# Ten of 22 feed-forward tile pairs by Strassen's seven products, and the inner width in three parts

## The chip, the cores and the metric

The kernel runs on one core of a Trainium2 chip. The metric is the device time of one execution in microseconds; the time before is the median of three runs.

## The reference, cut to what matters

The input has 512 positions of width 1024. A first block (three mixers and a convolutional feed-forward) is followed by a second block of two layers. Each of these layers has a feed-forward, a mixing stage and another feed-forward, so that the gated feed-forward below is computed four times, with an inner width `D_FF` of 2816:

```python
def _swiglu(x, w_in, w_out):
    a, b = jnp.split(x @ w_in, 2, axis=-1)
    return (jax.nn.silu(a) * b) @ w_out

n = _modulate(_rmsnorm_2(h, norm_g[l, 0]), mod[:, 0, 0], mod[:, 0, 1])
h = h + 0.5 * mod[:, 0, 2] * _swiglu(n, ffn_w_in[l, 0], ffn_w_out[l, 0])
# ... mixing stage ...
n = _modulate(_rmsnorm_2(h, norm_g[l, 2]), mod[:, 2, 0], mod[:, 2, 1])
h = h + 0.5 * mod[:, 2, 2] * _swiglu(n, ffn_w_in[l, 1], ffn_w_out[l, 1])
```

`mod` is a product of a conditioning vector with a large matrix, and `_modulate(xn, shift, scale)` is `xn * (1 + scale) + shift`.

## The kernel before

Activations lie with features on the 128 partitions and 512 tokens along the free axis, as 8 chunks (`KD`) of 128 features. Each float32 product is made of three matmuls: both operands are split into a high and a low part, and `mm3` (L275) adds high by high (L277), high by low (L278) and low by high (L279). A weight tile of 128 outputs comes by `weight` (L262): SyncE issues a 512 KB transfer into one of three `raw` buffers, ScalarE rounds it to `hi` (L268), VectorE subtracts for `lo` (L272); `hi` and `lo` have four buffers each. `dense` (L281) multiplies such a tile by all 512 tokens: 8 chunks x 3 = 24 matmuls of 512 columns.

`swiglu` (L729) norms its input into `xh` and `xl`, and then goes through the 22 tile pairs (`NF`) of the inner width: a gate tile and a value tile by `dense`, Silu on ScalarE (L740), the product on VectorE (L741), and the split into chunk f of `hh` and `hl` (L344, L346). The first two pairs come by `dense_halves` (L292), which does the first 256 tokens for all four weight tiles and then the other 256, so that work can start when the norm of the first half is there. When all 22 chunks stand, `outputs` (L303) makes the 8 output tiles over 22 chunks each, and adds them to the residual `res` through the gate (L726). The last output tile (the last two where there are at most 8 chunks) is done by token halves, and between them stand the reductions and the `rsqrt` chain of the next norm's first half (`part`, L465): the per-token sums of squares (L425), some ten small VectorE operations (L375 to L400) and the spread of the result over the partitions (L433). `scaled` (L489) then applies the next norm: per chunk and half one product into `nm` (L498), a high part on ScalarE (L503) and a low part on VectorE (L504). In the first feed-forward `joint_norm` (L755) also scales the residual itself (L766).

The modulation matrix is read in 144 tiles of 512 KB; each is one VectorE operation (L1436). They are queued in `self.mods`, and `filler` pops some between other work with a low priority. In `swiglu` one is popped for each pair, and two for each of the first five output tiles.

The order of the instructions on each engine is made by the framework's scheduler: a lower program position goes first, an instruction that could run goes before one that still waits, and waits are put where data or buffers need them. PSUM has three banks of tag `acc`, two of `s`, two of `t` and one of `o`.

## Time and profile before

| | us |
|---|---|
| median of three runs | 3364.63 (3364.01 to 3367.19) |
| the profiled execution | 3369.15 |
| its span | 3367.0 |
| TensorE busy (share of the span) | 3289.3 (98%) |
| VectorE busy | 1902.2 (56%) |
| ScalarE busy | 1345.2 (40%) |
| GpSimd busy | 133.5 (4%) |

The profile is of one execution. A busy time is the union of an engine's instructions; matmuls overlap in the records, so that the distance of two starts, not a duration, is the price of one. The four feed-forwards of the second block begin at about 1091, 1859, 2228 and 2987 us of the span and take some 365 us each. In a row of a timeline the first number is the start and the second the duration, in us; a name such as `acc<-xh,hi` gives the output, the moving operand and the weights.

### The profile page before, as it was taken

To read this page: it belongs to the slowest core of one execution; us is meant where nothing else is said; L and a number is where in the kernel's file an instruction comes from. 1 tells how busy PE (TensorE), PEld (TensorE's weight loads), DVE (VectorE), ACT (ScalarE), POOL (GpSimd) and SP (SyncE) were. 2 spreads that over 40 slices of the span, in tenths; PEclk is the share of its full clock that TensorE was granted. 3 is DMA by queue.
4 is the path that set the end of the run, shared out by engine and by line. 5 is a ranking of instruction groups with operands and counts; after the bars stand their busy time and mean duration, and the time that the engine had idled before them with its cause. 6 is when DMAs were issued, how large, how long until landed. Compare 5 with 4: busy or idle time off the path is not lost.

```text
span 3367.0 us, 43228 instructions
## 1 busy us (share of the span) xinstructions
PE 3289.3 (98%) x16598; PEld 2739.1 (81%) x16598; DVE 1902.2 (56%) x3598; ACT 1345.2 (40%) x2363; POOL 133.5 (4%) x152
## 2 busy tenths in 40 slices
PE   8999998899999999999999999999999999999998
PEld 6779777688888888897887888898888878888887
DVE  6757685777764644458556644454444775553333
ACT  4646664444433332247632322232222673232221
POOL 0000121000000000021000000000000200000000
PEclk9999999999999999999999999999999999999999
DMA  5351225444454444431245444434443212523332
GB/s 176 96 147 36 80 91 176 155 150 160 134 168 132 132 144 143 138 113 51 73 127 189 138 138 147 142 124 144 144 149 124 81 57 85 174 89 95 99 93 71
DMA packets 143641, 412.89 MB, mean 123 GB/s; under 512 B 27749, under 2 KB 32677, under 8 KB 142922
## 3 DMA queue, kind: packets, MB, share of 16 engines
q1 hardware_dynamic: 142248, 408.02, 38.1%
q8 instruction: 130, 2.13, 0.3%
q0 software_dynamic: 896, 1.87, 0.2%
q14 instruction: 77, 0.63, 0.1%
q10 hardware_dynamic: 290, 0.24, 0.0%
HBM read 383.06 MB, written 27.01 MB: 122 GB/s over the span
## 4 chain that ended last, share of the span: by engine, by line
PE 85%; DVE 5%; ACT 4%; DMA 2%; issue 1%; POOL 0%; SPq 0%; DVEq 0%; ACTq 0%; POOLq 0%
PE acc L277 24%; PE acc L278 24%; PE acc L279 24%; PE o L822 2%; PE s L783 1%; PE t L810 1%; ACT hi L268 1%; PE s L278 1%; PE s L277 1%; PE s L279 1%; DMA raw<-in_ada_dram 1%; DVE lo L272 1%; PE t L425 1%; ACT sq L1507 1%; DMA gt<-gd 1%
## 5 line engine op out<-in xcount | busy, mean ns | idle before, releaser
L277 PE MATMUL acc<-xh,hi 128*128 128x512 f32 (+1 forms) x2872 | 1084.5, 381 | 13.9 <-ACT gst L627 3.6
L268 ACT ACTIVATE hi<-raw 128x1024 fp32r<-128x1024 f32 (+2 forms) x529 | 541.5, 1025 | 1388.9 <-PE acc L278 1279.1
L278 PE MATMUL acc<-xl,hi 128*128 128x512 f32 (+1 forms) x2872 | 1089.9, 382 | 4.7 <-DVE xl L348 3.1
L279 PE MATMUL acc<-xh,lo 128*128 128x512 f32 (+1 forms) x2872 | 1087.0, 381 | 0.5 <-DVE lo L272 0.5
L272 DVE TENSOR_TENSOR lo<-raw,hi 128x1024 fp32r<-128x1024 f32 (+2 forms) x493 | 590.2, 1198 | 476.9 <-ACT hi L268 453.6
L277 PEld LDWEIGHTS acc<-xh,hi 128*128 128x128 f32 x2872 | 541.5, 190 | 116.8 <-ACT gst L627 5.6
L278 PEld LDWEIGHTS acc<-xl,hi 128*128 128x128 f32 x2872 | 543.4, 190 | 105.2 <-issue 5.3
L279 PEld LDWEIGHTS acc<-xh,lo 128*128 128x128 f32 x2872 | 542.9, 189 | 98.6 <-issue 4.0
L1436 DVE CUSTOM_DVE_ANT_0 raw<-raw,sc,vp 128x1024 f32<-128x1024 f32 x144 | 184.8, 1284 | 274.9 <-DMA raw<-in_ada_dram 274.4
L279 PE MATMUL acc<-hh,lo 128*128 128x512 f32 (+1 forms) x880 | 338.0, 384 | 0.0
L278 PE MATMUL acc<-hl,hi 128*128 128x512 f32 (+1 forms) x880 | 334.5, 380 | 0.0
L277 PE MATMUL acc<-hh,hi 128*128 128x512 f32 (+1 forms) x880 | 333.0, 378 | 0.0
L278 PEld LDWEIGHTS acc<-hl,hi 128*128 128x128 f32 x880 | 165.2, 188 | 37.9
L277 PEld LDWEIGHTS acc<-hh,hi 128*128 128x128 f32 x880 | 165.1, 188 | 34.7
L279 PEld LDWEIGHTS acc<-hh,lo 128*128 128x128 f32 x880 | 165.5, 188 | 33.3
L741 DVE TENSOR_TENSOR g<-g,acc 128x512 f32<-128x512 f32 x84 | 57.8, 688 | 219.1 <-PE acc L279 218.4
L270 POOL TENSOR_TENSOR lo<-raw,hi 128x1024 fp32r<-128x1024 f32 (+3 forms) x36 | 77.2, 2148 | 2093.5 <-ACT hi L268 1982.5
L726 DVE SCALAR_TENSOR_TENSOR res<-acc,mod,res 128x512 f32<-128x512 f32 (+1 forms) x48 | 33.9, 707 | 116.0 <-PE acc L279 116.0
L346 DVE TENSOR_TENSOR ptl<-t,pth 128x512 fp32r<-128x512 f32 (+3 forms) x148 | 81.6, 567 | 26.8 <-ACT pth L344 26.1
L787 ACT ACTIVATE pr<-pr,mx 128x128 f32<-128x128 f32 (+3 forms) x160 | 88.5, 555 | 15.6 <-DVE mx L786 14.8
L344 ACT ACTIVATE pth<-t 128x512 fp32r<-128x512 f32 (+3 forms) x148 | 70.7, 497 | 44.5 <-PE t L810 37.1
L786 DVE CUSTOM_DVE_ANT_0 pr<-s,cm 128x128 f32<-128x128 f32 (+3 forms) x160 | 74.5, 485 | 22.2 <-PE s L783 17.7
(522 smaller groups left out, 4167.1 us busy)
## 6 DMA issues: line engine op xcount, KB each, us to landing
raw<-in_w_in_dram SPq DMA_DIRECT2D x176, 512.0 KB, 3.6
raw<-in_ada_dram SPq DMA_DIRECT2D x144, 512.0 KB, 3.5
raw<-in_w_out_dram SPq DMA_DIRECT2D x64, 512.0 KB, 3.6
raw<-in_w_mix_dram SPq DMA_DIRECT2D x56, 512.0 KB, 3.5
raw<-in_w_up_dram SPq DMA_DIRECT2D x44, 512.0 KB, 3.7
gd<-gst SPq DMA_DIRECT2D x56, 256.0 KB, 2.0
gt<-gd SPq DMA_DIRECT2D x56, 256.0 KB, 3.2
raw<-in_w_gate_dram SPq DMA_DIRECT2D x24, 512.0 KB, 4.3
```

What stands on the lines that cost most here:

```text
L268: self.last_act = nc.scalar.activation(hi[:, :n], raw[:, :n], AF.Copy)
L270: nc.gpsimd.tensor_sub(lo[:, :n], raw[:, :n], hi[:, :n].bitcast(F32))
L272: nc.vector.tensor_sub(lo[:, :n], raw[:, :n], hi[:, :n].bitcast(F32))
L277: return [mm(acc, ahi, bhi, start=start, stop=False, **kw), mm(acc, ahi, blo, start=False, stop=False, **kw), mm(acc, alo, bhi, start=Fals ...
L278: mm(acc, ahi, blo, start=False, stop=False, **kw),
L279: mm(acc, alo, bhi, start=False, stop=stop, **kw)]
L344: nc.scalar.activation(hi, src, AF.Copy, scale=scale)
L346: nc.vector.tensor_sub(lo, src, hi.bitcast(F32))
L786: nc.vector.tensor_tensor_reduce(p, ps[:, :w], mask(i), -scale, 3.0e38, op0=OP.add, op1=OP.min, accum_out=mx[:, i:i + 1])
L787: nc.scalar.activation(p, p, AF.Exp, bias=mx[:, i:i + 1], scale=-1.0, accum_out=sm[:, i:i + 1])
L822: nc.tensor.matmul(acc[:, j * P:], x, m, start=start and j == 0 and k == 0, stop=stop and j == 3 and k == len(ops) - 1)
L1436: nc.vector.tensor_tensor_reduce(w, w, self.sc, 1.0, self.v("ada_b_2", l * 72 + n), op0=OP.mult, op1=OP.add, accum_out=self.mod[:, l, n:n ...
```

## The change

In each of the four feed-forwards the inner width is cut into three parts of 8, 8 and 6 chunks (`PARTS`). After each part its down products run at once over that part's chunks and are added to the residual, so that `hh` and `hl` have 8 chunks instead of 22. Where a part isn't the last, each of its 8 output tiles is made by `dense`, and two modulation tiles are popped behind each; none are popped in the pairs any more. The last part goes through `outputs`, over 6 chunks, which brings it under the rule for two output tiles in halves.

Of the 22 pairs, those with odd f from 3 on (ten) go through `seven`. It takes the gate and the value tile as a two by two block matrix (gate or value, first or second four chunks of the input) and the input as another (chunks, token halves), and makes Strassen's seven products of half size: 4 chunks by 256 columns each, 12 matmuls. Sums of the weights are made on VectorE in the `raw` buffers, sums of the input once for a feed-forward in `sums`, from the normed values that `scaled` now leaves in `xb` (`keep`). Combining the products takes two banks of `s` and two of `t` and further VectorE operations.

```diff
@@ scaled
             for k in range(n):
-                if b - a == S or k % 2 == 0:
-                    m2 = self.t(self.np_, [P, S], F32, "nm", 2)
-                m = m2 if b - a == S else m2[:, k % 2 * (b - a):(k % 2 + 1) * (b - a)]
+                if self.keep is not None:
+                    m = self.keep(k, a)
+                else:
+                    if b - a == S or k % 2 == 0:
+                        m2 = self.t(self.np_, [P, S], F32, "nm", 2)
+                    m = m2 if b - a == S else m2[:, k % 2 * (b - a):(k % 2 + 1) * (b - a)]
@@ swiglu
+    PARTS = ((0, 8), (8, 16), (16, 22))
+    PLAIN = 3
+    H = S // 2
...
         with tc.tile_pool(name="ffn", bufs=1) as pool:
+            th = t(pool, [P, 4, 4, H], F32R, "th")
+            tl = t(pool, [P, 4, 4, H], F32R, "tl")
+            xb = [t(pool, [P, 4, H], F32, n, 3) for n in ("sh", "sh", "sl", "sl")]
+            self.keep = lambda k, a: xb[k // 4 * 2 + (a > 0)][:, k % 4]
             norm()
-            hh = t(pool, [P, NF, S], F32R, "hh")
-            hl = t(pool, [P, NF, S], F32R, "hl")
-            for f in range(NF):
-                if f == 0:
-                    accs = self.dense_halves([src_in[0], src_in[NF], src_in[1], src_in[NF + 1]])
-                ga, va = (accs.pop(0) if accs else self.dense(src_in[n], KD, self.xh, self.xl) for n in (f, NF + f))
-                g = t(pool, [P, S], F32, "g", 2)
-                nc.scalar.activation(g, ga, AF.Silu)
-                nc.vector.tensor_mul(g, g, va)
-                self.split(hh[:, f], hl[:, f], g)
-                self.filler(1, self.mods)
-            self.outputs(src_out, NF, hh, hl, self.residual(gate), None, 2)
+            self.keep = None
+            hh = t(pool, [P, 8, S], F32R, "hh")
+            hl = t(pool, [P, 8, S], F32R, "hl")
+            accs = self.dense_halves([src_in[0], src_in[NF], src_in[1], src_in[NF + 1]])
+            self.sums(xb, th, tl, shift4)
+            for p, (f0, f1) in enumerate(self.PARTS):
+                for f in range(f0, f1):
+                    i = f - f0
+                    if f < self.PLAIN or f % 2 == 0:
...
+                    else:
+                        self.seven(pool, src_in[f], src_in[NF + f], th, tl, hh[:, i], hl[:, i])
+                kc = f1 - f0
+                cols = slice(f0 * P, f1 * P)
+                down = [src_out[n][:, cols] for n in range(KD)]
+                if p < len(self.PARTS) - 1:
+                    put = self.residual(gate)
+                    for n in range(KD):
+                        acc = self.dense(down[n], kc, hh, hl)
+                        put(n, slice(0, S), acc)
+                        self.filler(2, self.mods)
+                else:
+                    self.outputs(down, kc, hh, hl, self.residual(gate), None, 2)
@@ new
+    def sums(self, b, th, tl, shift4):
+        nc, H = self.nc, self.H
+        s1, s2 = shift4(0), shift4(4)
+        ds = self.t(self.np_, [P, 4], F32, "ds", 1)
+        nc.vector.tensor_sub(ds, s2, s1)
+        nc.vector.tensor_sub(b[0], b[0], b[1])
+        nc.vector.tensor_sub(b[2], b[3], b[2])
+        nc.vector.tensor_add(b[2], b[2], b[0])
+        stt = nc.vector.scalar_tensor_tensor
+        for k in range(4):
+            stt(b[1][:, k], b[3][:, k], ds[:, k:k + 1], b[1][:, k], op0=OP.add, op1=OP.subtract)
+            stt(b[3][:, k], b[3][:, k], s2[:, k:k + 1], b[0][:, k], op0=OP.add, op1=OP.add)
+        self.split(th[:, 0], tl[:, 0], b[0])
+        self.split(th[:, 3], tl[:, 3], b[3], -1.0)
+        self.split(th[:, 1], tl[:, 1], b[1])
+        self.split(th[:, 2], tl[:, 2], b[2])
...
+    def seven(self, pool, src_g, src_v, th, tl, hi, lo):
+        nc, t, H = self.nc, self.t, self.H
+        ra, rb = self.raw(src_g), self.raw(src_v)
+        W = self.WN
+        g1, g2, v1, v2 = ra[:, :W // 2], ra[:, W // 2:], rb[:, :W // 2], rb[:, W // 2:]
...
+        ah, al = parts(self.wp, ("hi", "lo"), ra, 4)
+        bh, bl = parts(self.wp, ("hi", "lo"), v2, 4)
+        nc.vector.tensor_add(v2, v1, v2)
+        nc.vector.tensor_add(v1, g1, v1)
+        nc.vector.tensor_add(g1, v2, g1)
+        nc.vector.tensor_add(g2, g1, g2)
+        ch, cl = parts(pool, ("sh", "sl"), ra, 3)
+        dh, dl = parts(pool, ("sh", "sl"), rb, 3)
+        def product(acc, wh, wl, half, xs):
+            for k in range(4):
+                s = slice(half * (W // 2) + k * P, half * (W // 2) + (k + 1) * P)
+                self.mm3(acc, wh[:, s], wl[:, s], xs[0][:, k], xs[1][:, k], k == 0, k == 3)
...
+        p17, p26 = self.bank("s"), self.bank("s")
+        p45, p3 = self.bank("t"), self.bank("t")[:, :H]
+        v = t(self.np_, [P, S], F32, "nm", 2)
+        q = t(pool, [P, H], F32, "q", 2)
+        g = t(pool, [P, S], F32, "g", 2)
+        product(p17[:, :H], ah, al, 0, X(0, 0))
+        product(p17[:, H:], dh, dl, 0, T(1))
+        product(p26[:, :H], ah, al, 1, X(1, 0))
+        product(p26[:, H:], ch, cl, 0, T(3))
+        y = t(self.np_, [P, S], F32, "sqa")
+        nc.scalar.activation(y, p17, AF.Copy)
+        add(two(g), twice(y[:, :H]), two(p26))
+        add(q, g[:, H:], y[:, H:])
+        product(p45[:, :H], bh, bl, 0, T(2))
+        product(p45[:, H:], dh, dl, 1, T(0))
+        add(two(v), twice(q), two(p45))
+        product(p3, ch, cl, 1, X(1, 1))
+        add(g[:, H:], g[:, H:], p45[:, H:])
+        add(g[:, H:], g[:, H:], p3)
+        nc.scalar.activation(g, g, AF.Silu)
+        nc.vector.scalar_tensor_tensor(g, v, -1.0, g, op0=OP.mult, op1=OP.mult)
+        self.split(hi, lo, g)
```

## Rows read from the trace of the kernel before

**Rows 1.** Windows: length, busy time (count) by engine, granted clock, DMA share, GB/s

```profile
core 0: us, PE busy (x) PEld busy (x) DVE busy (x) ACT busy (x) POOL busy (x), PEclk, DMA share, GB/s
1118.20:1458.00 339.80, 339.80 (x1545) 281.27 (x1544) 149.72 (x195) 93.63 (x115) 1.46 (x1) 1.00 0.45 143
...
3012.00:3350.00 338.00, 338.00 (x1530) 279.47 (x1529) 110.89 (x129) 89.61 (x110) 0.00 (x0) 1.00 0.30 89
...
1094.00:1097.00 3.00, 3.00 (x16) 3.00 (x16) 3.00 (x12) 1.71 (x5) 0.00 (x0) 0.50 0.02 7
...
2985.00:3013.00 28.00, 27.46 (x226) 27.05 (x225) 22.01 (x54) 14.97 (x27) 0.00 (x0) 1.00 0.25 77
```

**Rows 2.** Timeline of TensorE, first feed-forward: start, duration, engine, line, tiles, shape

```profile
1115.31 0.28 PE L277 MATMUL s<-xh,hi 128*128 128x256 f32 x1
...
1118.19 0.40 PE L277 MATMUL acc<-xh,hi 128*128 128x512 f32 x1
...
1129.09 0.39 PE L277 MATMUL acc<-xh,hi 128*128 128x512 f32 x1
```

**Rows 3.** Timeline of TensorE, down products of the first feed-forward

```profile
1340.03 0.39 PE L277 MATMUL acc<-hh,hi 128*128 128x512 f32 x1
...
1347.03 0.39 PE L277 MATMUL acc<-hh,hi 128*128 128x512 f32 x1
```

**Rows 4.** Timeline of TensorE, second half of the last output tile there

```profile
1456.84 0.28 PE L277 MATMUL s<-hh,hi 128*128 128x256 f32 x1
...
1460.44 0.28 PE L277 MATMUL s<-hh,hi 128*128 128x256 f32 x1
```

**Rows 5.** Groups by form, 1075 to 3367 us, VectorE, then ScalarE: busy us, mean ns

```profile
L272 DVE TENSOR_TENSOR lo<-raw,hi 128x1024 fp32r<-128x1024 f32 x319 | 390.3, 1223 | 289.6 <-ACT hi L268 272.2 <-PE acc L1690 8.4
L1436 DVE CUSTOM_DVE_ANT_0 raw<-raw,sc,vp 128x1024 f32<-128x1024 f32 x103 | 132.3, 1284 | 247.2 <-DMA raw<-in_ada_dram 247.2
L346 DVE TENSOR_TENSOR hl<-g,hh 128x512 fp32r<-128x512 f32 x88 | 60.3, 685 | 0.0
...
L498 DVE SCALAR_TENSOR_TENSOR nm<-res,gs,o 128x256 f32<-128x256 f32 x40 | 17.7, 473 | 2.3 <-PE o L433 2.3
...
L346 DVE TENSOR_TENSOR ptl<-t,pth 128x256 fp32r<-128x256 f32 x32 | 13.5, 421 | 1.9 <-ACT pth L344 1.5
...
L268 ACT ACTIVATE hi<-raw 128x1024 fp32r<-128x1024 f32 x335 | 355.4, 1061 | 1036.7 <-PE acc L278 984.0 <-PE s L278 22.6 <-issue 12.9
L344 ACT ACTIVATE hh<-g 128x512 fp32r<-128x512 f32 x88 | 55.5, 631 | 8.9 <-DVE g L741 8.9
L740 ACT ACTIVATE g<-acc 128x512 f32<-128x512 f32 x88 | 51.3, 582 | 2.6 <-PE acc L279 2.6
```

**Rows 6.** Timeline of VectorE, start of the first feed-forward

```profile
1104.73 5.96 DVE L766 SCALAR_TENSOR_TENSOR res<-res,vp,t 128x256 f32<-128x256 f32 x15
...
1113.30 1.22 DVE L272 TENSOR_TENSOR lo<-raw,hi 128x1024 fp32r<-128x1024 f32 x1
```

**Rows 7.** Timelines of VectorE and of TensorE, start of the last feed-forward

```profile
3000.09 1.27 DVE L504 SCALAR_TENSOR_TENSOR xl<-nm,mod,xh 128x256 fp32r<-128x256 f32 x3
...
3012.48 0.40 PE L277 MATMUL acc<-xh,hi 128*128 128x512 f32 x1
```

**Rows 8.** Timeline of TensorE, first output tiles behind the first mixing

```profile
1818.84 0.39 PE L279 MATMUL acc<-xh,lo 128*128 128x512 f32 x1
1819.07 0.39 PE L278 MATMUL acc<-xl,hi 128*128 128x512 f32 x1
```

**Rows 9.** Timeline of VectorE, end of the first feed-forward

```profile
1451.74 0.48 DVE L726 SCALAR_TENSOR_TENSOR res<-acc,mod,res 128x256 f32<-128x256 f32 x1 [5.18 <-PE acc L279]
...
1456.80 1.26 DVE L498 SCALAR_TENSOR_TENSOR nm<-res,gs,o 128x256 f32<-128x256 f32 x3 [1.14 <-PE o L433]
...
1461.51 0.47 DVE L726 SCALAR_TENSOR_TENSOR res<-s,mod,res 128x256 f32<-128x256 f32 x1
```

**Rows 10.** Timeline of VectorE, last norm of the kernel

```profile
3351.09 3.22 DVE L752 SCALAR_TENSOR_TENSOR res<-res,vp,o 128x256 f32<-128x256 f32 x8 [1.14 <-PE o L433]
```

**Rows 11.** DMA issues of the page: KB each, median us from issue to landing

```profile
raw<-in_w_out_dram SPq DMA_DIRECT2D x64, 512.0 KB, 3.6
```

28 lines of the change are left out of this document (25 added, 3 removed).

## The prediction

> **What bounds the kernel now.** I read the busy shares of the page first, where TensorE leads, then the windows of the feed-forwards, then the starts of the matmuls. From the first full-width matmul of a feed-forward to its last columns TensorE is busy for all of the window at full clock [rows 1]: 339.8 of 339.8 us in the first, 338.0 of 338.0 in the last. VectorE is busy for 149.7 and 110.9 us of those windows, ScalarE for about 90. So these stages are matmul time and nothing else: what the change takes from the matmul stream is gained, unless something else becomes late.
>
> **The price of a matmul.** Starts, not durations, count, since records overlap. In [rows 2] 24 matmuls of 256 columns take 1118.19 - 1115.31 = 2.88 us, 0.120 each; the next 48 of 512 columns take 1129.09 - 1118.19 = 10.90 us, 0.227 each, and these 48 are one plain tile pair. Two halves cost 0.240, so halving the columns loses 13 ns per whole matmul. Down products that move hh cost 7.00 us for 30 [rows 3], 0.2333 each, but at 256 columns 3.60 us for 30 [rows 4], again 0.120. I take 0.120 for all of the seven products, whichever tile they move.
>
> **The pairs.** A pair by `seven` has 7 x 4 x 3 = 84 matmuls of 256 columns: 84 x 0.120 = 10.08 us against 48 x 0.2267 = 10.88. That is 0.80 us a pair; ten pairs (f = 3, 5, ... 21) in four feed-forwards give 40 x 0.80 = **32.0 us**. The arithmetic saving of 12.5% is 7.4% in time. The Trainium skill (TensorE: Matmul & The Clock Gate, "Back-to-back issue gap") gives a matmul its columns at 2.4 GHz plus about 2.5 ns; by it the pair would go from 10.4 to 9.2 us and the change would take some 47 us off. The trace does not agree, with 13 ns instead of 2.5, and the rows decide.
>
> **The down products.** 528 a feed-forward, before and after. The last output tile ran in halves over 22 chunks (132 of 256 columns), now two tiles over 6 chunks (72): 462 x 0.2333 + 132 x 0.120 = 123.6 us before, 492 x 0.2333 + 72 x 0.120 = 123.4 after. Gain 4 x 0.2 = **0.8 us**. The smaller hh could lie where the moving operand is read as fast as xh; then 492 matmuls gain 0.0067 each, 3.3 us a feed-forward, 13 in all. Nothing says it does, so I take 0 and keep -13 as an end.
>
> **VectorE in the pair stage.** From the grouped durations [rows 5] a plain pair costs two 1024-wide lows (2 x 1.22), a product and a low of 512 (0.69 each): 3.8 us. A pair by `seven` costs three lows of 1024 and one of 512 (4.35), four weight sums of 512 (2.74), and behind the products four operations of 512 and three of 256 (4 x 0.69 + 3 x 0.42 = 4.0): 11.1 us, more than its matmuls. But plain pairs stand between: 14.9 us of VectorE for 10.9 + 10.1 = 21.0 of TensorE, 71%. The modulation loads (1.28 each, [rows 5]) leave this stage for the down products. The preparation of the next `seven` can start when the first products of the present one have freed their weight buffers (4.3 us in) and has until 21.0, some 16.7 us, in which VectorE owes it 7.1, the closing of the present pair 4.0 and the plain pair 3.8. It fits with about 2 us to spare. I take 1 us in all, with 0 to 45 as ends (first rival).
>
> **The start of each feed-forward.** This is the dearest new work. `sums` runs on VectorE between the norm and the weights of pair 2: three operations of 1024 (3.7), eight of 256 at 0.47 (3.8), four lows (4.9): 12.4 us, where nothing stood. In the first feed-forward the scaling of the residual ends at 1104.73 + 5.96 = 1110.7, and the low of pair 2's weights, now at 1113.3 [rows 6], moves behind `sums` and the closing of pairs 0 and 1, to about 1126; TensorE wants it at 1118.2. In the last, the norm ends at 3001.4 and pair 2 starts at 3012.5 [rows 7]. Wanted are 12.4 + 1.2 = 13.6 us after the norm's end, there are 7.5, 11.1, and by the same reading 12 and 8 in the second and third: short by 6, 2.5, 1.6 and 5.6 us, 16 in all. Part of it is absorbed: the order of the matmuls is not fixed to high-high, high-low, low-high. In [rows 8] a low-high is followed by the high-low of another step while the last chunk is waited for. 16 of the 24 matmuls of a weight tile need no low part, 3.6 us, and the first products of pair 3 need only the first preparation. I take half, **8 us**, ends 2 and 23.
>
> **The end of each feed-forward.** The norm of the first token half hides behind the second half of the last output tiles. In [rows 9] the first half's last column is taken up at 1451.74 and the norm starts at 1456.80, 5.1 us later, while the last residual update of the second half is at 1461.51: TensorE had 66 matmuls, 7.9 us, and the reductions. With 36 matmuls it has 4.3 plus 0.8, so cover falls by 3.6 us. Where the mixing follows (twice), only two weight tiles are worked on and VectorE paces the norm, so I charge 3 us each. Where a feed-forward follows, four tiles give 11.5 us of work a half, and I charge 0.5; modulation work that lands in between, 0.5. The mixing itself ends with 48 matmuls in the second half and its window shows 0.5 us of idle TensorE [rows 1]. **7 us**, ends 3 and 14. In the last norm, the first half's eight operations of 3.2 us [rows 10] now run beside the second half's chain instead of before it: **1 us**, ends 0 and 3.
>
> **The rest.** Going from pairs to down products happens 12 times instead of 4, each time behind a pair by `seven` whose closing is some 3.4 us after its last product (0.42 + 0.58 + 0.69 + 0.63 + 0.69 [rows 5] and hops); the down tile has 5 or 7 chunks of work before it needs that pair, 3.5 to 4.9 us. Nothing is charged; without the cover it is at most 3.4 x 12. Sixteen more residual updates a feed-forward, of the size of the 0.69 rows, lie beside matmuls. Two modulation loads now stand with each 5.6 us down tile (39 tiles have them): three transfers in 5.6 us through three raw buffers. A weight holds its buffer for 3.6 us of landing [rows 11] and 1.06 + 1.22 of splitting, a modulation load for 3.6 + 1.28; the average is 5.2. It fits barely: **2 us**, ends 0 and 35.
>
> **The sum.** 32.0 + 0.8 - 1 - 8 - 7 - 1 - 2 = 13.8 us. On the profiled execution's own time of 3369.15 (span 3367.0 and 2.15 around it) that is 3355.4; this execution lies 4.5 us over the median of 3364.63, and on the median it is 3350.8. I forecast **3351 us**. What a measurement of this kernel can tell from no change is about 0.2%, 6.7 us: faster is under 3357.9, slower over 3371.4.
>
> **Rivals.**
> First, slower: VectorE's order lets the weight sums come late. If the closing of one pair by `seven` (ending about 13 us after its start) goes ahead of all preparation of the next, then 13 + 7.1 + 2.4 for the plain pair's lows and about 1.5 of waits for ScalarE end at 24 us, against 22.4 when the first sums are wanted: 1.6 us for each of the 28 that follow another closely, 45 us, **3396**. It turns the result from 0.5 us per such pair. For it speak the 71% and that VectorE's load of 11.1 exceeds the pair's 10.1; against it that the order in the trace takes ready work early. The Trainium skill (TensorE: Matmul & The Clock Gate, table of the specification) says that VectorE's queue is strictly first in, first out; by it a late closing holds every preparation queued behind it.
> Second, no change: the start is not absorbed and the clock falls. Then 16 us are lost instead of 8, and where TensorE has idled it runs at a granted 0.50 (1.2 GHz) for some us, as at the start of the first feed-forward, where 16 matmuls took 3 us [rows 1]; at 2 us for each start, **3365**.
> Third, the down products become as quick as those of xh: **3338**.
> Fourth, the modulation loads and weights collide in the down products, 0.3 to 0.9 us on 39 tiles: 12 to 35 us, around **3370**.
>
> **Chances.** Forecast 0.50 (its own range 3338 to 3361), first rival 0.17, second 0.15, third 0.08, fourth 0.10. Faster by over 0.2%: 0.46 of the forecast, 0.08 of the third, 0.04 of the others, 0.58. Within: 0.20. Slower: the first, and 0.05 of the fourth, 0.22. The range 3333 to 3385 leaves out most of the first rival above (0.13) and some 0.05 at either extreme of the others.
>
> **What would show it.** Right: 84 starts 0.120 apart in each pair by `seven`, windows of the pair stage full on TensorE, VectorE near 70%, idle TensorE only at the first 30 us of a feed-forward and at its end. The first rival shows as TensorE waiting for lows of sh/sl or sums of raw in the middle of the stage; the second as long waits for lo before pair 2 and a granted clock under 1 there; the third as 0.227 in down products; the fourth as waits for lo released by transfers there. The forecast is wrong if 256-column products take more than 0.127 us, where the whole gain of the pairs would be down to 8 us.

## The result, and the profile after

| | before | after |
|---|---|---|
| median of four runs, us | 3365.91 (3364.01 to 3370.20) | 3405.45 (3402.64 to 3408.87) |
| span of the profiled execution, us | 3367.0 | 3405.1 |
| granted TensorE clock, mean | 0.992 | 0.982 |

The ratio is 1.0114, 95% interval 1.0101 to 1.0126: the change makes the kernel 1.1% slower, some 39 us. The forecast was 3351, with a range up to 3385.

Windows of the changed kernel: two pair stages, then the down products of three parts, 192 matmuls each. The columns are those of [rows 1].

```profile
core 0: us, PE busy (x) PEld busy (x) DVE busy (x) ACT busy (x) POOL busy (x), PEclk, DMA share, GB/s
1235.80:1319.40 83.60, 83.60 (x530) 76.08 (x529) 58.40 (x80) 32.94 (x42) 0.00 (x0) 1.00 0.38 121
1370.90:1433.60 62.70, 62.70 (x397) 57.02 (x396) 44.24 (x61) 23.91 (x31) 0.00 (x0) 1.00 0.38 122
1185.90:1235.50 49.60, 46.26 (x194) 37.24 (x193) 31.64 (x44) 9.63 (x10) 0.00 (x0) 0.97 0.64 209
1319.40:1370.60 51.20, 47.36 (x194) 37.99 (x193) 33.41 (x47) 9.63 (x10) 0.00 (x0) 0.93 0.67 214
2482.80:2527.20 44.40, 44.40 (x194) 36.07 (x193) 16.18 (x19) 8.70 (x9) 0.00 (x0) 1.00 0.27 83
```

The pair stages are as forecast. The first row is four plain pairs and four by `seven`: 4 x 10.88 + 4 x 10.08 = 83.84 us worked out, 83.6 measured, TensorE full, clock 1.00. The second is three and three, 62.88 and 62.7. VectorE is busy for 70% of both. So the 32 us of the pairs are there. The down products differ: the last row, which holds no modulation work, takes 44.4 us for 192 x 0.2333 = 44.8. The two above it, with such work, take 49.6 and 51.2.

The waits of TensorE over the second block, first the changed kernel, then the one before. The columns are the total us, the number of waits and the longest.

```profile
PE acc L278 <- ACT hh L345: 21.0, 7, 3.8
PE s L278 <- DVE g L760: 9.2, 4, 6.0
PE acc L279 <- DVE xl L508: 7.7, 6, 2.9
```

```profile
PE t L425 <- ACT sq L461: 3.2, 5, 1.2
PE o L822 <- DVE ptl L346: 3.0, 2, 1.6
PE acc L278 <- DVE xl L504: 1.3, 2, 0.9
```

The first two are new, the third has grown from 1.3 us, and each has a place. `hh` is waited for at the **entry** into a down product, `g` at the **start** of a feed-forward, `xl` at the start of a **mixing**. To price them I take the distances of matmul starts and subtract 0.120, 0.2267 or 0.2333 us for each [rows 2 to 4]. What is left is time lost to a wait, or to the granted 0.50 that follows one.

| where | lost before, us | lost after, us |
|---|---|---|
| entries into 12 down products | 0 | 34.5 (seven of them, 4.0 to 6.8 each) |
| starts of the four feed-forwards | 5.3, 5.0, 0.2, 1.5 | 12.9, 3.8, 6.5, 5.4 |
| starts of the two mixings | 6.9, 7.0 | 16.9, 17.1 |

New losses are 34.5 + 16.6 + 20.1 = 71.2 us, and 1.7 at the last norm. With the 33 us gained that leaves +40. The spans differ by 38.1; the part ahead of the second block happened to be 2.7 us shorter in this execution. By the clock records of the two traces the granted clock is 0.50 for 91 us behind 1060 us in the changed kernel (27 of them in the seven entries, 34 in the two mixings) and for 20 in the one before. Where TensorE is full, 71 us more at half the rate cost 35 us; by this estimate about half of the new losses is clock, and the rest is the waits themselves.

### The profile page after: what moved, and what is told of

It is laid out like the page before. It is cut to its first block, busy times and chain, and to the rows that moved or that the text cites. A ratio compares the mean times of both kernels' runs of the same rounds, so it can differ in the third digit from the quotient of the medians.

```text
span 3405.1 us, 46671 instructions
## 1 busy us (share of the span) xinstructions
PE 3286.9 (97%) x17918; PEld 2797.5 (82%) x17918; DVE 2277.8 (67%) x4176; ACT 1450.3 (43%) x2503; POOL 128.5 (4%) x150
## 4 chain that ended last, share of the span: by engine, by line
PE 80%; DVE 10%; DMA 5%; ACT 4%; issue 1%; SPq 0%; POOL 0%; ACTq 0%; DVEq 0%; POOLq 0%
PE acc L278 20%; PE acc L279 19%; PE acc L280 19%; PE s L279 2%; PE s L280 2%; PE s L278 2%; DMA raw<-in_w_out_dram 2%; DVE lo L273 2%; PE o L932 2%; PE s L893 2%; PE t L280 1%; PE t L278 1%; PE t L279 1%; ACT hi L269 1%; PE t L920 1%
## 5 line engine op out<-in xcount | busy, mean ns | idle before, releaser
L279 PE MATMUL acc<-xl,hi 128*128 128x512 f32 (+1 forms) x2232 | 845.1, 382 | 9.2 <-DVE xl L508 7.7
L278 PE MATMUL acc<-xh,hi 128*128 128x512 f32 (+1 forms) x2232 | 838.5, 381 | 13.8 <-ACT gst L631 3.6
L269 ACT ACTIVATE hi<-raw 128x1024 fp32r<-128x1024 f32 (+3 forms) x449 | 456.3, 1017 | 918.7 <-PE acc L279 571.8
L280 PE MATMUL acc<-xh,lo 128*128 128x512 f32 (+1 forms) x2232 | 843.5, 381 | 3.0 <-DVE lo L273 3.0
L278 PEld LDWEIGHTS acc<-xh,hi 128*128 128x128 f32 x2232 | 424.0, 192 | 91.5 <-issue 6.9
L279 PEld LDWEIGHTS acc<-xl,hi 128*128 128x128 f32 x2232 | 426.7, 192 | 82.3 <-DVE xl L508 8.7
L280 PEld LDWEIGHTS acc<-xh,lo 128*128 128x128 f32 x2232 | 426.7, 192 | 78.5 <-issue 5.7
L1546 DVE CUSTOM_DVE_ANT_0 raw<-raw,sc,vp 128x1024 f32<-128x1024 f32 x144 | 183.7, 1282 | 51.7 <-DMA raw<-in_ada_dram 51.3
L279 PEld LDWEIGHTS acc<-hl,hi 128*128 128x128 f32 x880 | 169.0, 192 | 36.7
L278 PE MATMUL s<-xh,hi 128*128 128x256 f32 x448 | 127.3, 284 | 9.2 <-DVE g L760 9.2
L279 PE MATMUL s<-xl,hi 128*128 128x256 f32 x448 | 127.7, 285 | 0.0
L280 PE MATMUL s<-xh,lo 128*128 128x256 f32 x448 | 126.9, 283 | 0.0
```

The costliest lines, as they stand in the source:

```text
L269: self.last_act = nc.scalar.activation(hi[:, :n], raw[:, :n], AF.Copy)
L278: return [mm(acc, ahi, bhi, start=start, stop=False, **kw), mm(acc, ahi, blo, start=False, stop=False, **kw), mm(acc, alo, bhi, start=Fals ...
L279: mm(acc, ahi, blo, start=False, stop=False, **kw),
L280: mm(acc, alo, bhi, start=False, stop=stop, **kw)]
L1546: nc.vector.tensor_tensor_reduce(w, w, self.sc, 1.0, self.v("ada_b_2", l * 72 + n), op0=OP.mult, op1=OP.add, accum_out=self.mod[:, l, n:n ...
```

## One entry, instruction by instruction

The changed kernel, end of the first part. First ScalarE, then SyncE's queue of transfers, then VectorE, then TensorE: start, duration, line, tiles, and in brackets the idle time before and what ended it.

```profile
1184.63 1.06 ACT L269 ACTIVATE hi<-raw 128x1024 fp32r<-128x1024 f32 x1 [4.79 <-DMA raw<-in_w_out_dram]
1191.12 1.06 ACT L269 ACTIVATE hi<-raw 128x1024 fp32r<-128x1024 f32 x1 [5.43 <-DMA raw<-in_w_out_dram]
1192.08 0.61 ACT L852 ACTIVATE g<-g 128x512 f32<-128x512 f32 x1
1194.07 0.63 ACT L345 ACTIVATE hh<-g 128x512 fp32r<-128x512 f32 x1 [1.38 <-DVE g L853]
...
1181.93 1.84 SPq L1545 DMA_DIRECT2D raw<-in_ada_dram  x2
1186.97 0.33 SPq L266 DMA_DIRECT2D raw<-in_w_out_dram  x1
1188.18 0.33 SPq L1545 DMA_DIRECT2D raw<-in_ada_dram  x1
...
1185.72 1.23 DVE L273 TENSOR_TENSOR lo<-raw,hi 128x1024 fp32r<-128x1024 f32 x1 [1.25 <-ACT hi L269]
1189.00 1.28 DVE L1546 CUSTOM_DVE_ANT_0 raw<-raw,sc,vp 128x1024 f32<-128x1024 f32 x1
1190.20 0.42 DVE L851 TENSOR_TENSOR g<-g,t 128x256 f32<-128x256 f32 x1
1193.35 0.69 DVE L853 SCALAR_TENSOR_TENSOR g<-nm,g 128x512 f32<-128x512 f32 x1
...
1191.03 0.39 PE L279 MATMUL acc<-hl,hi 128*128 128x512 f32 x1
1194.75 0.78 PE L278 MATMUL acc<-hh,hi 128*128 128x512 f32 x1 [3.34 <-ACT hh L345]
...
1197.04 0.63 PE L278 MATMUL acc<-hh,hi 128*128 128x512 f32 x1
1197.47 0.63 PE L279 MATMUL acc<-hl,hi 128*128 128x512 f32 x1
...
1198.28 0.40 PE L279 MATMUL acc<-hl,hi 128*128 128x512 f32 x1
```

The last pair's products ended at 1185.9. Its Silu (L852) could have begun at 1190.6, when L851 had made its input. It began at 1192.08, since ScalarE stood at the split of a later down weight, whose transfer had only been issued at 1186.97, behind modulation tiles. L851 itself was late: VectorE took a low of that kind and modulation operations (L1546) between the closing operations. TensorE ran out of chunks at 1191.4, waited 3.34 us, and then its starts lay 0.43 apart instead of 0.233 until 1198.28, at a granted clock (third number from the end) of 0.50:

```profile
1195.00:1198.00 3.00, 3.00 (x8) 2.35 (x9) 0.85 (x3) 0.00 (x0) 0.00 (x0) 0.50 0.77 273
```

The same step at the second part of the third feed-forward, with no modulation tiles near. Silu and split follow their inputs at once, and TensorE doesn't wait:

```profile
2483.95 0.64 ACT L852 ACTIVATE g<-g 128x512 f32<-128x512 f32 x1 [2.81 <-DVE g L851]
2485.35 0.63 ACT L345 ACTIVATE hh<-g 128x512 fp32r<-128x512 f32 x1 [0.76 <-DVE g L853]
```

## Experiments on the entries

My theory from these rows: modulation tiles crowd the entry. Rivals: the closing of a pair by `seven` is too long in itself; or VectorE's modulation operations, not the transfers. Line numbers of the experiments' kernels are shifted by a few lines. The table gives for every kernel the nine down products of the first three feed-forwards (us from first to last start; 44.4 and, for a last part, 34.4 to 35.0 without loss) and the sum of what they lose. The fourth feed-forward loses nothing in any.

| kernel | ratio to before | nine down products | lost |
|---|---|---|---|
| changed | 1.0114 | 49.5 51.2 38.9, 49.5 48.9 38.9, 49.4 44.4 34.9 | 34.5 |
| a1 loads in pairs, last parts kept theirs | 1.0067 | 44.4 44.4 43.8, 44.4 44.4 44.3, 44.4 44.5 44.1 | 27.5 |
| a2 all pairs plain | 1.0065 | 46.3 47.3 36.9, 46.3 46.5 38.2, 49.6 44.6 35.4 | 20.0 |
| a3 small VectorE operation | 1.0067 | 49.4 48.8 37.0, 45.5 46.8 39.0, 48.5 44.4 35.0 | 23.3 |
| a4 no transfer | 1.0029 | 44.4 44.4 36.7, 44.4 44.4 39.2, 44.4 44.4 35.0 | 6.2 |
| c1 all loads in pairs | 1.0089 | 44.4 44.7 35.2, 45.6 44.4 34.4, 44.6 44.5 34.9 | 1.6 |
| d4 loads away | 1.0044 | 44.4 44.4 35.0, 44.4 44.4 34.4, 44.4 44.5 35.2 | 0.2 |
| e1 ScalarE's order | 1.0071 | 47.1 46.4 36.3, 46.9 48.3 40.5, 47.1 44.4 34.9 | 20.8 |
| e2 VectorE's order | 1.0137 | 48.0 50.1 42.9, 47.4 49.0 46.9, 49.4 44.4 35.0 | 42.0 |
| e3 both orders | 1.0137 | 46.9 52.3 43.6, 47.5 50.3 46.1, 49.1 44.4 34.9 | 44.0 |

**Loads back behind the pairs.**

```diff
                     else:
                         self.seven(pool, ...)
+                    self.filler(1, self.mods)
...
                         put(n, slice(0, S), acc)
-                        self.filler(2, self.mods)
```

> The changed kernel, with the modulation loads back where they stood before: one behind each tile pair, none in the down products of the first two parts. In the trace of the changed kernel seven of the twelve entries into down products lose 3.9 to 6.7 us each (TensorE waits for hh, then runs at a granted 0.50), some 34 us in all, and all seven are in parts that carry modulation loads; the others run in 44.6 us against 49 to 51. Theory 1 (the loads that crowd the entry are the cause): the seven losses go, the time falls from 3405 by 28 to 36 us, to about 3371, and the pair stages stay at 0.120 and 0.2267 a matmul. Rival (the entry itself, the closing of a pair by seven, is the cause, and the loads only fall beside it): the entries go on losing 3 us and more, the time stays above 3395. Second rival (VectorE cannot take the loads in the pair stage, at 71% plus 1.28 for each pair of 10.5 us): the entries are mended but the pair stages stretch, 0.5 us for each pair, and the time stays near 3400.

Measured 3390.74, ratio 1.0067 (1.0050 to 1.0083). The first two parts are mended as the theory says, and the pair stages stay at 83.7 and 62.7 us. But the last parts, which kept ten tiles each, now lose about 9 us each instead of 4, 4 and 0: the crowd moved there, and the gain is half of what was expected.

**The parts alone.**

```diff
-    PLAIN = 3
+    PLAIN = 22
...
-            self.sums(xb, th, tl, shift4)
```

> The parts alone: the changed kernel with all 22 tile pairs plain, without the sums at the start of the feed-forward; three parts, down products and modulation loads as in the changed kernel. The pair stages give back their 32 us. Theory 1 (entries crowded by modulation loads, longer ends): entries lose about as much as in the changed kernel, 25 to 34 us, the ends 15 to 20, the starts nothing: about 3365 + 45 = 3410. Rival (the closing of a pair by seven is what makes the entries late): a plain pair closes about 2 us sooner, the entries lose under 10 us in all, and the time is 3380 to 3390.

Measured 3390.96, 1.0065 (1.0049 to 1.0082), between the two. The entries lose 20 us though a plain pair closes sooner. So the longer closing adds to the loss (34.5 against 20) where loads stand near; by itself it costs nothing, as the entries without loads show, at the end of the changed kernel's third feed-forward, in its fourth, and in d4 below. The pairs can be priced here too: from the last down product of one part to the first of the next, eight plain pairs take 87.3 us and six 65.6, the changed kernel's four and four 83.9 and its three and three 63.0, so a pair by `seven` saves some 0.85 us, worked out as 0.80.

**Small operation, and no transfer.**

```diff
# a3: lite is 1 in the down products of the first two parts
-            nc.vector.tensor_tensor_reduce(w, w, self.sc, ...
+            z = 16 if self.lite else D
+            nc.vector.tensor_tensor_reduce(w[:, :z], w[:, :z], self.sc[:, :z], ...
# a4: likewise
-            nc.sync.dma_start(w, A["ada"][l, n])
-            nc.vector.tensor_tensor_reduce(w, w, self.sc, ...
+            if not self.lite:
+                nc.sync.dma_start(w, A["ada"][l, n])
+            nc.vector.tensor_tensor_reduce(w, self.sc if self.lite else w, self.sc, ...
```

> The changed kernel; in the down products of the first two parts each modulation load is made as before, but the VectorE operation behind it reads 16 of its 1024 columns (so these modulation values are not the reference's). It takes VectorE's 1.28 us operations away and leaves the transfers and their places in the raw ring. Theory 1 (transfers: SyncE issues the down weights late, since the raw ring of three is shared, and ScalarE, which works in order, stands at the split of a weight that has not landed while the silu of the last pair waits behind it): the entries still lose most of their 34 us, time 3390 to 3405. Rival (VectorE: its modulation operations stand between the closing operations of the last pair): the entries lose little, time 3370 to 3380.

> The changed kernel; in the down products of the first two parts the modulation operation on VectorE is kept at full size, on values that already lie in the core, and takes its place in the raw ring, but the transfer of 512 KB is left out (so these modulation values are not the reference's). Theory 1 (transfers late, ScalarE stands at the split of a weight): the entries are mended, time 3368 to 3380. Rival (VectorE's operations between the closing operations): the entries lose as before, time 3395 to 3405. A mixture would show as a gain here and in the run with the tiny operation whose sum is about 34 us.

Measured 3394.34, 1.0067 (1.0049 to 1.0085), and 3377.20, 1.0029 (1.0018 to 1.0040). Both edits act in the first two parts alone. There the entries lose 26.5 us in the changed kernel, nothing without the transfers, and 17 with the small VectorE operation. The transfers are the larger cause; the loss needs them, and VectorE's operations add to it.

**Every load behind a pair.**

```diff
+                    self.filler(2 - f % 2, self.mods)      # behind every pair; none in down products
...
-                    self.outputs(down, kc, hh, hl, self.residual(gate), None, 2)
+                    self.outputs(down, kc, hh, hl, self.residual(gate))
```

> The changed kernel with every modulation load of a feed-forward behind a tile pair (two behind an even pair, one behind an odd one) and none in any down product, the last part's included. In the run with one load behind each pair the first two parts entered without loss (44.4 us each) but the last part, which kept its ten loads, lost 9.2 to 9.8 us in three feed-forwards: ScalarE stood 5 us at the split of a down weight that had not landed, with the silu of the last pair behind it. Theory 1 (loads in front of the entry): those 28 us go too, 3390.7 - 28, about 3362, all twelve entries without wait. Rival (VectorE, now up to 14.9 + 3.8 us of 21.0 in the pair stage, makes lows late): pair stages stretch beyond 83.8 and 62.8 us, and the time stays over 3375.

Measured 3397.56, 1.0089 (1.0072 to 1.0106): the entries lose 1.6 us in all, as the theory says, and yet the time is worse than with a1. The loss went to the starts: 23.0 us in the first feed-forward and 13.8 in the third. SyncE's queue and TensorE's longest wait there:

```profile
1107.95 0.33 SPq L1545 DMA_DIRECT2D raw<-in_ada_dram  x1
1121.43 2.74 SPq L266 DMA_DIRECT2D raw<-in_w_in_dram  x2
...
PE acc L278 <- ACT hi L269: 12.2, 1, 12.2
```

Nothing is issued for 13.5 us: modulation tiles hold the ring of `raw` buffers, since their VectorE operations stand behind `sums`, and pair 2's weights come late. The pair stages of eight with 1.5 loads a pair took 84.6 to 85.4 us, 1 to 1.7 more.

**Loads away from entries and starts.**

```diff
+                    self.filler(int(f > self.PLAIN), self.mods)   # pairs from the fifth on; none in down products
...
# conv_ffn, the feed-forward of the first block
-                self.filler(1, self.mods)
+                self.filler(2, self.mods)
```

> The changed kernel with the modulation loads taken from the down products, from the first four pairs and from the last output tiles of these feed-forwards: one behind each pair from the fifth on, and two instead of one behind each pair of the feed-forward of the block before. In the run with all of them behind the pairs all twelve entries were mended, but the first feed-forward's start lost 23 us instead of 12.9, 12.2 of it in one wait for the high part of a weight: the loads stood there in the raw ring ahead of the next weight. Theory (a load costs where a weight behind it in the ring is wanted at once, at the entry and at the start alike): entries without loss and starts as in the changed kernel, 3405 - 34, about 3371. Rival (the feed-forward of the block before has no room for 22 more loads, or the pairs have not): waits there, and a time over 3380.

Measured 3380.68, 1.0044 (1.0027 to 1.0060). All entries are whole, and the gain is 24 us, not 34: the first block's feed-forward ended 2 to 15 us later than in the kernel before in the profiles of the four kernels with this edit (8 in this one), and 17 modulation tiles were left to be made between 2943 and 2996 us, ahead of the last feed-forward. Kernels whose first block is unchanged differ by some 9 us at that point, so that the small end of the 2 to 15 shows nothing.

**Which queue holds the chain.** The loads stay where the change put them. From the third down tile on, the split of a weight is issued behind the split of the last pair's `hh` on ScalarE (e1), or lows and modulation operations behind that of `hl` on VectorE (e2), or both (e3).

```diff
+    def later(self, i):
+        return nullcontext() if self.behind is None else self.tc.issue_after(self.behind[i].ins)
...
+        with self.later(0):                          # e1, e3
             self.last_act = nc.scalar.activation(hi[:, :n], raw[:, :n], AF.Copy)
...
+            with self.later(1):                      # e2, e3; the modulation operation likewise
                 nc.vector.tensor_sub(lo[:, :n], raw[:, :n], hi[:, :n].bitcast(F32))
```

> The changed kernel with every load where it was; only ScalarE's order at the entry into a part's down products is given: the splits of the down weights from the third tile on are issued behind the split of the last pair's hh. In the changed kernel ScalarE stood 5.4 us at such a split, its transfer not landed, while the silu of the last pair was queued behind it. Theory A (ScalarE's queue decides): the seven entries lose 0 to 1.5 us instead of 3.9 to 6.7, the time falls by 24 to 32 us to about 3377. Theory B (VectorE's queue decides: there a low of the same weight and the modulation operations, each waiting for its transfer, stand between the closing operations): the gain is under 8 us.

> The changed kernel with only VectorE's order at the entries given: the modulation operations, and the lows of the down weights from the third tile on, are issued behind the low of the last pair's hl. ScalarE's order is left to the planner. Theory A (ScalarE's queue decides): the gain is under 8 us, unless the planner now moves ScalarE's splits too. Theory B (VectorE's queue decides): the entries are mended, 24 to 32 us, about 3377.

> Both orders given. If each queue alone holds the closing chain, only this run mends the entries: 3405 - 30, about 3375, as the run without the transfers (3377). If the raw ring of three itself is short, since the modulation loads now hold their places until the closing is done, the second and third down tiles wait for their weights instead, 2 to 4 us at each entry, and the gain is under 15 us.

Measured 3393.11, 1.0071 (1.0056 to 1.0085); 3415.24, 1.0137 (1.0123 to 1.0152); 3417.78, 1.0137 (1.0122 to 1.0152). Neither theory holds alone. With ScalarE's order mended the entries lose 20.8 instead of 34.5, and what is left is VectorE: in e1 ScalarE now idles for the input of its Silu, while VectorE waits for a modulation tile to land and works two of them off between the closing operations (first ScalarE, then VectorE):

```profile
1195.60 0.63 ACT L863 ACTIVATE g<-g 128x512 f32<-128x512 f32 x1 [10.95 <-DVE g L862]
...
1191.75 1.28 DVE L1557 CUSTOM_DVE_ANT_0 raw<-raw,sc,vp 128x1024 f32<-128x1024 f32 x1 [2.17 <-DMA raw<-in_ada_dram]
1193.89 1.28 DVE L1557 CUSTOM_DVE_ANT_0 raw<-raw,sc,vp 128x1024 f32<-128x1024 f32 x1
1195.09 0.42 DVE L862 TENSOR_TENSOR g<-g,t 128x256 f32<-128x256 f32 x1
```

With VectorE's order mended as well, the modulation tiles keep their `raw` buffers until the closing is done, and the next weights can't be fetched. In e2 10.6 us pass over the issue of two modulation tiles on SyncE's queue, and the down products wait for lows all the way through, 32 times:

```profile
1313.06 10.60 SPq L1556 DMA_DIRECT2D raw<-in_ada_dram  x2
...
PE acc L285 <- DVE lo L278: 14.6, 32, 1.2
```

So the ring of three is what is short, as far as these runs go; no run gives it a fourth buffer, which would be the direct test. ScalarE and VectorE both stood at operations whose tiles had not come, with closing operations behind them, and the closing chain passes both.

## Experiments on the starts and on the mixings

**Sums after the plain pairs.**

```diff
-            self.sums(xb, th, tl, shift4)          # ahead of the loop
...
+                    if f == self.PLAIN:
+                        self.sums(xb, th, tl, shift4)
```

> The changed kernel with the preparation of the sums placed after the three plain pairs in the program instead of ahead of them; nothing else. In the changed kernel the first feed-forward's start loses 12.9 us of wait and slow clock, where the parts with plain pairs alone lose 2.6; the longest wait, 6 us, is for the multiplication of pair 1, which stands on VectorE behind the sums. Theory (VectorE's order, sums ahead of the closings and of pair 2's low): the four starts win 10 + 2 + 3 + 3 us, 3405 falls to 3385 to 3395. Rival (the sums are wanted by the first pair by seven and come late there instead): the wait moves 11 us on, to the first products with th and tl, and the time stays within 5 us of 3405.

Measured 3385.52, 1.0049 (1.0032 to 1.0066). The four starts lose 6.1, 1.5, 3.8 and 1.5 us instead of 12.9, 3.8, 6.5 and 5.4, 15.7 less. What had been late is in the changed kernel's VectorE and TensorE rows:

```profile
1109.00 1.23 DVE L783 TENSOR_TENSOR sh<-sh,sh 128x1024 f32<-128x1024 f32 x1
...
1118.98 1.22 DVE L349 SCALAR_TENSOR_TENSOR tl<-sl,th 128x1024 fp32r<-128x1024 f32 x1
1120.71 0.69 DVE L760 TENSOR_TENSOR g<-g,s 128x512 f32<-128x512 f32 x1
1121.31 1.22 DVE L273 TENSOR_TENSOR lo<-raw,hi 128x1024 fp32r<-128x1024 f32 x1
...
1121.45 0.58 PE L278 MATMUL s<-xh,hi 128*128 128x256 f32 x1 [6.03 <-DVE g L760]
```

`sums` holds VectorE from 1109.00 to 1120.1. TensorE's order had the first product of the first pair by `seven`, which needs a bank of `s`, ahead of the rest of pair 2; that bank is free only when pair 1's product (L760) is made, and this stands behind `sums`. After the edit the longest wait at this start is 0.8 us, for the low part of a later weight.

**GpSimd's lows later.** In the mixing GpSimd makes the low part of some of the weights.

```diff
+        self.spare = False
         accs = self.dense_halves([W[0], W[1]])
...
+            self.spare = True
             ahead = queries(0)
```

> The changed kernel with GpSimd's share of the weights' low parts beginning only after the first compressed keys of the mixing, so that the first weights' lows go to VectorE; nothing else. In the changed kernel, in both mixings, one 256-wide operation of VectorE in the norm takes 2.4 us and one 4.1 us, against 0.4 to 0.5 elsewhere, each ending with GpSimd's low (2.36 us) beside it. Theory (the two engines hold each other up at what they share): without GpSimd's low the long operations are 0.5 us, each mixing's start wins 4 to 6 us, and 3405 falls to 3393 to 3398. Rival (the length is a wait for something else that the row does not show, or VectorE's own two lows of 1.2 us take the place): the time stays within 4 us of 3405.

Measured 3389.74, 1.0059 (1.0043 to 1.0075). The changed kernel's rows of VectorE and of GpSimd, and then VectorE's answering rows in this run:

```profile
1471.51 2.38 DVE L464 TENSOR_TENSOR sqa<-sqa,sq 128x256 f32<-128x256 f32 x1
1475.77 4.12 DVE L508 SCALAR_TENSOR_TENSOR xl<-nm,mod,xh 128x256 fp32r<-128x256 f32 x1
...
1471.25 2.36 POOL L271 TENSOR_TENSOR lo<-raw,hi 128x1024 fp32r<-128x1024 f32 x1 [9.20 <-ACT hi L269]
1477.25 2.35 POOL L271 TENSOR_TENSOR lo<-raw,hi 128x1024 fp32r<-128x1024 f32 x1
```

```profile
1472.42 0.42 DVE L464 TENSOR_TENSOR sqa<-sqa,sq 128x256 f32<-128x256 f32 x1
1475.41 0.48 DVE L508 SCALAR_TENSOR_TENSOR xl<-nm,mod,xh 128x256 fp32r<-128x256 f32 x1
```

Each long operation ended 0.3 us after GpSimd's, and both are short without it. The mixings' starts lose 13.2 and 13.1 us instead of 16.9 and 17.1: 7.7 us. The time fell by more, 18 us by the ratios; from the start of the second block on the profiles differ by 14.5. The rest lies at the entries, which lose 28.0 us in this profile instead of 34.5 (31.4 in b1) although neither edit touches them: a few us there shift with any edit. The Trainium skill (SBUF — State Buffer, "SBUF: two separate sides") says that VectorE with two operands in SBUF and GpSimd share a pair of ports, held by one of them for a whole instruction. The rows agree so far as both operations have two such operands and end with GpSimd's; that the second began 1.5 us ahead of GpSimd's low is not explained by it. The kernel before had met this once in each mixing, for 0.8 us over three operations, as its VectorE rows and GpSimd's show:

```profile
1457.98 2.04 DVE L504 SCALAR_TENSOR_TENSOR xl<-nm,mod,xh 128x256 fp32r<-128x256 f32 x3
...
1468.88 1.27 DVE L504 SCALAR_TENSOR_TENSOR xl<-nm,mod,xh 128x256 fp32r<-128x256 f32 x3
...
1456.54 2.40 POOL L270 TENSOR_TENSOR lo<-raw,hi 128x1024 fp32r<-128x1024 f32 x1 [806.79 <-ACT hi L268]
```

That the changed kernel meets it so much more is not a matter of time alone. `weight` gives a low to GpSimd by the parity of a counter that every allocated tile and bank raises, a modulation tile too:

```python
        if self.spare and self.n % 2:
            nc.gpsimd.tensor_sub(lo[:, :n], raw[:, :n], hi[:, :n].bitcast(F32))
```

So in kernels that allocate the same otherwise, the number of modulation tiles made up to a mixing decides which lows GpSimd makes there. The changed kernel has made 81 at the first mixing and 144 at the second. GpSimd makes three lows around the last down product there: 12.8 and 1.2 us ahead of its start and 4.8 behind it. It makes the same three in c1's second mixing (144 tiles) and in d4's first (79). In a1 (72 and 143), in c1's first (72) and in d4's second (123) the number differs by an odd one, and GpSimd makes a single low, 9.0 us ahead. From the start of the last down product to the first product on `kh`, a step inside the mixing, the kernel before takes 57 us, the mixings with three lows 65.2 to 68.3 and those with one 58.1 to 59.3. For the first mixing of the kernel before, of the changed kernel and of a1 that last product starts at 1460.7, 1472.5 and 1467.1; the first product on `kh` in each, and a1's single low:

```profile
1517.72 0.36 PE L783 MATMUL s<-kh,qs 128*128 128x256 f32 x1
1540.13 0.36 PE L893 MATMUL s<-kh,qs 128*128 128x256 f32 x1
1525.22 0.36 PE L893 MATMUL s<-kh,qs 128*128 128x256 f32 x1
...
1458.06 2.38 POOL L271 TENSOR_TENSOR lo<-raw,hi 128x1024 fp32r<-128x1024 f32 x1 [809.69 <-ACT hi L269]
```

With the same cover as the changed kernel a1 is 1 us over the kernel before at each mixing, and the changed kernel 11. So by these runs the larger part of the loss at the mixings goes with the parity, which the change flipped by chance, and little with the cover. No run flips the parity alone.

**Edits together.** c2 is c1 with these two; d1 is d4 with them; d2 adds a longer cover at the ends; d3 is d4's place for the loads and GpSimd's later lows with all pairs plain.

```diff
# d2
-    PARTS = ((0, 8), (8, 16), (16, 22))
+    PARTS = ((0, 7), (7, 14), (14, 22))
...
-        last = range(KD - (2 if kc <= 8 else 1), KD)
+        last = range(KD - (halves or (2 if kc <= 8 else 1)), KD)   # halves is 3 in these feed-forwards
```

> All three edits together: modulation loads behind the pairs, sums after the plain pairs, GpSimd's lows later. If the causes are separate and these three, the gains add: 3362 - 15 - 9, about 3338, the pairs' 32 us then showing against the kernel before. Rival (VectorE is full in the pair stage of the first pairs by seven, where sums, modulation operations and closings now meet): waits there, and a time of 3350 to 3365.

> The same with the sums after the three plain pairs and GpSimd's lows later in the mixing. Alone these two gave 20 and 16 us as timed, of which their traces show about 17 and 8 in the places they touch. Theory (three separate causes): 3371 - 17 - 8, about 3346, faster than the kernel before by what the pairs save less the ends. Rival (the loads' place decides all, and the others shift waits about): within 8 us of the run with the loads taken away alone.

> The same as the run with three edits, and a longer cover at the end of a feed-forward: parts of 7, 7 and 8 pairs, and the last three output tiles in halves, so that 72 matmuls of the second half (8.6 us) stand behind the first half's norm instead of 36 (4.3); the kernel before had 66. Theory (the ends cost 2 to 5 us each for want of cover): 4 to 12 us faster than that run. Rival (the ends' loss is VectorE's own chain of the second half, which no cover shortens, and 36 more matmuls in halves cost 13 ns each): within 3 us of it.

> The parts alone without what was found to cost: all 22 pairs plain, no sums, three parts; modulation loads taken away from the entries as above, GpSimd's lows later. Theory (what the parts themselves cost is the shorter cover at the ends): 2 to 10 us over the kernel before. By the run with three edits the ten pairs by seven then give 32 us less what the sums cost at the starts, 24 to 30. Rival (the entries lose even without the loads): over 12 us above the kernel before.

Measured: c2 3387.17, 1.0061 (1.0041 to 1.0081); d1 3362.72, 0.9988 (0.9978 to 0.9998); d2 3360.64, 0.9983 (0.9973 to 0.9993); d3 3396.39, 1.0085 (1.0068 to 1.0102). c2 keeps c1's fault, a wait of 13.6 us at the first start. d1 against d4 is 0.0056, 19 of the 25 us that the two edits had given in the places they touch. d2's longer cover gives little: from the last down product to the first product on `kh` d2 takes 57.5 and 57.9 us, d1 60.2 and 59.2, and the whole gained 2, within the intervals; that is the rival's range, not the theory's. d3 missed: the entries lose nothing, but in its profile the second block begins 15 us later than in the kernel before, and the stretch from the third feed-forward's last down product to the fourth's first takes 15 us more than in a2, which has the same pairs. Both are places where d4's edit puts loads, and d1 loses there too, some 9 us in each. Against d1 d3 prices the ten pairs by `seven` in place: 0.0097, 33 us, some of which is this difference.

**All edits at once.** e4 is e3 with sums late, GpSimd's lows late and d2's ends. f1 and f2 are d2 with its loads spread anew.

```diff
# f1: behind pairs from the fifth on; conv_ffn with one and two by turns
+                    self.filler((2 - f % 2) * (f > self.PLAIN), self.mods)
-                self.filler(1, self.mods)
+                self.filler(1 + (f % 2 or f == 0), self.mods)
# f2: behind pairs from the fifth on; conv_ffn as before the change
+                    self.filler((1 + (f % 4 != 3)) * (f > self.PLAIN), self.mods)
```

> All that the earlier runs pointed to, with the modulation loads where the change put them: both orders at the entries, sums after the plain pairs, GpSimd's lows later, parts of 7, 7 and 8 with the last three output tiles in halves. If the terms add: 3405 - 30 (entries) - 17 (starts) - 8 (GpSimd) - 9 (ends), about 3341, 0.7% under the kernel before. If what is won at one place is lost at the next, 3355 or more, as in the two runs that had moved the loads to the block before.

> The run with the loads taken away and the longer ends, its loads spread anew: two behind each even and one behind each odd pair from the fifth pair on, one and two by turns in the feed-forward of the block before. The former had run out of room and made 17 of them in one go ahead of the last feed-forward, and the block before ended some 9 us later in the profiles. Theory (a load is free where no wanted weight follows it): those 5 to 12 us come back, the pair stages lose 1 to 2 us each of the six that carry 1.5 loads a pair: 3343 to 3355. Rival (the loads cost about the same wherever they stand in the matmul stages): 3357 to 3365.

> The same with the feed-forward of the block before left at one load a pair, as in both kernels, and the loads of the second block's pairs raised to 1.75 a pair from the fifth on. VectorE then has 14.9 + 4.5 = 19.4 of 21.0 us in the pair stages. Theory (VectorE's room is used up there, first rival of the forecast): 0.3 us and more for each pair, 3355 to 3370. Rival (room is left): 3343 to 3355.

Measured: e4 3387.40, 1.0052 (1.0037 to 1.0067), with e3's starved ring: its down products take 40 us longer than d2's. f1 3354.66, 0.9964 (0.9950 to 0.9978), 12 us faster than the kernel before, at the upper end of what was expected. f2 3360.47, 0.9981 (0.9971 to 0.9990), 6 us. Two pair stages of eight in f1, with 1.5 loads a pair and with none:

```profile
1322.90:1409.70 86.80, 84.44 (x530) 76.23 (x529) 64.44 (x90) 33.62 (x43) 0.00 (x0) 1.00 0.49 153
...
3216.00:3299.70 83.70, 83.70 (x530) 76.10 (x529) 56.22 (x74) 34.26 (x43) 0.00 (x0) 1.00 0.34 107
```

At 1.5 a pair the loads cost 2.5 to 3 us in each such stage, where VectorE is busy for 74%. At one a pair, in a1 and d4, they cost the stage nothing: 84.0 us from the last down product of a part to the first of the next, 83.9 in the changed kernel. So the pairs take one load each for nothing, and none of the other places tried was free.

## Why the prediction failed

- **The pairs, -32: right.** 0.120 and 0.2267 held in every stage, and plain pairs instead cost 33 us (d3 against d1; 0.85 us a pair by the stages of a2). The down products cost 0.2333 as taken, so the third rival fell.
- **VectorE in the pair stage, 1: right** without loads (83.7 us, no wait), so the first rival did not happen. With one load a pair it is still nothing, with 1.5, which the change did not have, 1 to 3 us in eight pairs.
- **From pairs to down products, "nothing is charged": the step that failed.** The cover of 3.5 to 4.9 us was set against a closing of 3.4 us, added up from durations. That sum is right where nothing stands between: 3.2 us in the third feed-forward's second part, from 2482.8 to 2486.0. In the first it took 8.8, from 1185.9 to 1194.7, since its operations queue with splits, lows and modulation operations. The bound given, 3.4 us an entry and 41 in all, held the 34.5 only by luck: each of the seven entries with loads lost more than 3.4 (4.0 to 6.8), and five lost nothing.
- **Modulation loads in the down products, 2 (0 to 35): cause right, place wrong.** The fourth rival spread 12 to 35 us over 39 tiles. (The count was low: of the 103 modulation operations behind 1075 us [rows 5] 93 lie in or just ahead of down products in the changed kernel, two to a tile.) Past the entry no tile lost anything; the loads cost where the closing chain shares queues and ring with them. This and the step before are one loss, and I had charged them apart, one at nothing and one near its low end.
- **Start, 8 (2 to 23): mis-sized,** 16.6. The mechanism was `sums`, but the wait was for a PSUM bank behind pair 1's closing and not for the low of pair 2, which did come late.
- **Ends, 7 (3 to 14): mis-sized,** 20.1, above its own upper end and all at the mixings. The cover, of which the term was made, is the small part: a1, with the same cover, is 1 us over the kernel before at each mixing. The larger part goes with GpSimd's lows: 7.7 us came back when the first of them went to VectorE (b2), and some 10 at each mixing where the counter's parity gave GpSimd others (a1). I had no term for it, though the trace of before showed the two engines at it at 1457.98, next to the rows that I read for this step [rows 9].
- **Second rival.** Its mechanism, a wait and then the granted 0.50, is what entries, starts and mixings showed; it had been placed at the starts alone. (Its sum was 2 us short: 3351 + 8 + 4 x 2 is 3367.)
- **Last norm, 1:** 1.7.

With its own upper ends for the start, the ends, the loads and the entries the sum would have been 3350.8 + 15 + 7 + 33 + 41 = 3447; the measured 3405 lies between. I took each of four unknowns near its low end and let the range treat them as if they could not go wrong together. Two of them have a common cause, the entries and the loads: less time between dependent stages with the same work in the queues. At the mixings it was a side effect of the kernel's own bookkeeping.

## What to carry to other kernels

A stage boundary is priced by the closing chain as it runs, with all that stands in its in-order queues, not by the sum of its durations; list for each queue which transfers its next instructions wait for. Work that is "off the path" should be moved only with a look at where its buffers come from: three shared buffers tied the modulation tiles to every weight behind them, at an entry and at a start. Where several costs are bounded from both sides and share a cause, the range has to take them high together. And a choice that hangs on a counter, as GpSimd's lows do here, changes with every edit that allocates a tile; it is fixed by name before two kernels are compared.

## What the runs showed of the hardware

- A 256-wide VectorE operation with two operands in SBUF took 2.38 us in the changed kernel beside a GpSimd operation of 2.36 us, and 0.42 in b2, where GpSimd made no low there; another took 4.12 beside one of 2.35, and 0.48 in b2.
- After a wait of 3.34 us TensorE ran at a granted 0.50, its lower level of 1.2 GHz, for some 3.5 us: starts 0.43 us apart instead of 0.233. Such stretches are 91 us of the changed kernel behind 1060 us and 20 of the one before (ahead of it 31 in both), which is the mean granted clock of 0.982 against 0.992; the waits are paid for a second time in clock.
